# Weight blocks of a two-layer trunk step in two matmuls of 512 and 256 columns instead of three of 256

## The chip, the cores and the metric

The kernel runs on one core of one Trainium2 chip. The metric is the device time of one execution in microseconds; the median of three runs is given. The profile is that of one execution.

## What is computed

One inference step of a hybrid backbone with two layers over 128 context tokens and 128 latent tokens of width 2048, in float32. Each layer has a mixer (layer 0: differential attention beside a convolution module; layer 1: a state-space scan, S5, beside grouped attention) and a squared-ReLU MLP of width 8192, each behind a modulated RMS norm and with a gated residual. Cut to what matters here:

```python
def sq_relu_mlp(h, w1, w2):
    a = jax.nn.relu(h @ w1)
    return (a * a) @ w2

...
        xp = xp + gp1 * mp
        xs = xs + gs1 * ms
        xp = xp + gp2 * sq_relu_mlp(modulate(xp, norm_g[l, 1], sp2, cp2), mlp_w1[l], mlp_w2[l])
        xs = xs + gs2 * sq_relu_mlp(modulate(xs, norm_g[l, 1], ss2, cs2), mlp_w1[l], mlp_w2[l])
```

The linears are float32 products: the input and output projections of the mixers, the gate of the S5, and the two matrices of the MLP. The modulation (shift, scale and gate of each sub-layer) is a product of the conditioning vectors with a further weight matrix, `ada_w`.

## The kernel before

Activations lie transposed: 128 channels on the partitions, 256 columns (128 context tokens, then 128 latent tokens). A tile of 128 output channels is one linear. Its weights come as pieces of 128 x 1024 (eight blocks of 128 x 128), by SP's queue into eight `raw` buffers.

To keep float32 precision with the rounded type fp32r, every factor is split in two. `high` (line 359) rounds a weight piece on ACT into `wh`, `low` (line 364) has DVE subtract it from the piece into `wl`; there are four buffers of each. `put` (line 543) does the same with an activation tile: its high half goes to columns 0 to 255 of a tile `hl`, its low half to 256 to 511. A tile `hl` comes from a pool of 24 slots of 516 columns or, for part of the MLP's hidden activations, from the pool `hid`, whose tiles have 512 columns (line 549); in layer 1 all hidden tiles of the second quarter and the first eight of the others lie there, in layer 0 the first eight of each quarter (lines 1696, 1703, 1714).

`block` (line 453) is the product of one weight block with one activation tile, three matmuls into the same 256 columns of a PSUM bank:

```python
        mm(ps, w[0][:, s], x[:, 0:n], start=start, stop=False, **kw)
        mm(ps, w[0][:, s], x[:, n:2 * n], start=False, stop=False, **kw)
        mm(ps, w[1][:, s], x[:, 0:n], start=False, stop=stop, **kw)
```

`part` (line 460) runs it over the eight blocks of a piece, `linear` (line 476) over two pieces. There are other ways in: `staged` (line 482) runs a few linears side by side, first on one half of the activations; with 258 columns it serves the first linears of three norms (`enter`, line 769: 7, 5 and 7 linears), where two columns carry the shift. `pairs` (line 502) puts two linears in the halves of one bank (12 at the start of layer 0, 8 and 6 in the output projections). The gate of the S5 (`glu`, line 1192) has eight linears of eight blocks, every other one in a bank of the tag `ps`. `new` (line 472) hands out a bank of the tag `lin`, of which there are four, cut to 256 columns.

Results are taken out of PSUM by small strands: `copied` (line 557), `residual` (line 807: two DVE instructions that multiply by the gate and add to `x`, after a wait for the gate), `gated` (line 888: sigmoid of one linear times another), `u_tile` (line 1142), `glu_tile` (line 1179), `gqa_values` (line 1229), `gqa_head` (line 1253) and `squared_relu` (line 1735: ReLU on ACT into a tile `ms`, then one DVE product, then `put`).

The order of the instructions is planned. The program is many generators (strands). A first run, thrown away, keeps a clock for each engine by a table of costs (`charge`, line 136) and always goes on with a strand whose operands are there by then (`pick`, line 230); a second run issues in that order, loading and splitting weights ahead. `get` and `free` (lines 273, 285) count slots of named tags: four banks `lin`, three `ps`, three work tiles each of `h` and `xr`. Beside the linears run the modulation on TensorE (`ada`, line 569, in steps that fill gaps; `evict`, line 589, takes it out over a tile `ev`), two vectors of it on DVE (`ada_vector`, line 615, tile `va`, in both MLPs), the tables of the S5 (`s5_tables`, line 1404, in the first MLP: DVE products, transposes, DMAs from POOL's queue, `m2d` the last) and the convolution on DVE. Layer 0's MLP runs up and down projections by quarters; layer 1's runs up, up, down, down, up, down, up, down.

In time, the first mixer lasts to about 460 us, the first MLP to 1310, the second mixer to 1600, the second MLP to 2402, and the final norm ends the program.

Of the kernel before, what the change touches and what calls it, by code (L numbers as in the profile page):

```python
# [9 lines left out]
F32 = mybir.dt.float32  # L10
# [38 lines left out]
class Engine:  # L49
    """An engine whose instructions are also charged to the program's clocks."""  # L50
# [27 lines left out]
class Line:  # L78
    """A strand of the program: a generator that says what its next instructions wait for."""
# [4 lines left out]
    def on_pe(self):  # L84
        """Whether its next instructions are for TensorE."""
        return callable(self.wait) and getattr(self.wait, "pe", False)
# [25 lines left out]
class Kern:  # L112
    def __init__(self, ctx, tc, ins, outs, plan=None, order=None):
# [16 lines left out]
        self.cap = {"lin": 4, "ps": 3, "hl": 24, "h": 3, "xr": 3, "uv": 2}  # L130

# [1 line left out]
    # The program is many strands. A first run, that is thrown away, keeps a clock for each engine and always goes  # L133
    # on with a strand whose operands are there by then; the second run builds the program in that order, with
    # the weights loaded and split ahead of their use.
# [59 lines left out]
    def at(self, *aps):  # L195
        """When the tiles' contents are there."""
        return max([0] + [NEVER if v.tensor.name in self.held else self.at_.get(v.tensor.name, 0) for v in aps])

    def hold(self, t):
        """Not all of t is written yet."""  # L200
        self.held[t.tensor.name] = True
# [10 lines left out]
    def bulk(self, lead):  # L212
        """For work that is not urgent: the engines have come up to `lead` behind the clock of TensorE."""
# [59 lines left out]
    def get(self, *tags, on=None):  # L273
        """Waits for free slots (and for tiles), and takes them."""
# [55 lines left out]
    def source(self, spec):  # L330
        """The columns of a piece, side by side."""
# [38 lines left out]
    def pump(self, upto=0):  # L370
        """Loads ahead, as far as there is room, and splits what has come (and the pieces before `upto` in any
        case)."""
# [24 lines left out]
    def slot(self, key, bufs, back=0):  # L397
        """When the slot of the next tile (or one after it) is free."""
# [4 lines left out]
    def peek(self, n, split=False):  # L403
        """When the next n raw tiles are there."""
# [5 lines left out]
    def take(self, split, *spec):  # L410
        """The next piece that has been loaded: its halves, or itself."""
# [32 lines left out]
    def there(self, X, a, b, weights=True):  # L444
        """For a wait: the tiles X[a:b], and the weights that come next."""
# [7 lines left out]
    def block(self, ps, w, x, s, start, stop, **kw):  # L453
        mm = self.nc.tensor.matmul
        n = ps.shape[1]
        mm(ps, w[0][:, s], x[:, 0:n], start=start, stop=False, **kw)
# [3 lines left out]
    def part(self, ps, src, X, a, b, first, last, w=None, **kw):  # L460
        """ps (+)= weight blocks a to b of a tile times X[a:b]."""
# [10 lines left out]
    def new(self):  # L472
        yield from self.get("lin")
        return self.bank("lin")[:, 0:256]
# [7 lines left out]
    def staged(self, srcs, X, width, groups, done, release=None):  # L482
        """Linears in groups: first all on the half of X that is there first."""
        n = 0
# [1439 lines left out]
```

## Time and profile before

| what | before |
|---|---|
| runs, us | 2421.68, 2417.54, 2425.27 (median 2421.68) |
| profiled execution, span | 2417.9 us (the page gives no other time for it) |
| PE / weight loads / DVE / ACT / POOL busy | 96 / 88 / 70 / 48 / 7% of the span |
| matmuls, weight loads | 20152, 20152 |
| DMA moved | 627.64 MB, mean 260 GB/s |

Times within the execution are microseconds from the span's start. PE is TensorE's matmuls, PEld its weight loads, which run beside matmuls; the end of a matmul is modelled, so pitches are taken from one start to the next. All instructions of the kernel stand under one line (L60, the recording helper), so they are told apart by tile: `lin` is the bank that a linear writes, `wh` and `wl` the halves of its weights, `hl` of its activations.

### The profile page before, as it was taken

To read this page: it belongs to the slowest core of one execution; us is meant where nothing else is said; L and a number is where in the kernel's file an instruction comes from. 1 tells how busy PE (TensorE), PEld (TensorE's weight loads), DVE (VectorE), ACT (ScalarE), POOL (GpSimd) and SP (SyncE) were. 2 spreads that over 40 slices of the span, in tenths; PEclk is the share of its full clock that TensorE was granted. 3 is DMA by queue.
4 is the path that set the end of the run, shared out by engine and by line. 5 is a ranking of instruction groups with operands and counts; after the bars stand their busy time and mean duration, and the time that the engine had idled before them with its cause. 6 is when DMAs were issued, how large, how long until landed. Compare 5 with 4: busy or idle time off the path is not lost.

```text
span 2417.9 us, 49512 instructions
## 1 busy us (share of the span) xinstructions
PE 2331.7 (96%) x20152; PEld 2134.6 (88%) x20152; DVE 1696.8 (70%) x2957; ACT 1154.1 (48%) x1894; POOL 173.5 (7%) x293
## 2 busy tenths in 40 slices
PE   6999999999999999999999978999999999999997
PEld 1788887888999999999999857799999999999997
DVE  1489985677889898887666434566998855555555
ACT  2364457465444434434455644555744333443453
POOL 0000000000111011101000236000000000000000
PEclk9999999999999999999999988999999999999998
DMA  9979987879678898879877877765587855555552
GB/s 384 339 261 325 320 312 255 293 269 317 204 265 301 300 316 299 311 263 333 281 231 249 295 281 265 270 226 181 187 295 268 273 192 193 182 191 190 184 186 94
DMA packets 179638, 627.64 MB, mean 260 GB/s; under 512 B 21377, under 2 KB 21393, under 8 KB 179153
## 3 DMA queue, kind: packets, MB, share of 16 engines
q1 hardware_dynamic: 169920, 595.67, 71.1%
q0 software_dynamic: 9488, 28.81, 3.9%
q8 instruction: 158, 2.59, 0.4%
q14 instruction: 72, 0.58, 0.1%
HBM read 602.17 MB, written 26.41 MB: 260 GB/s over the span
## 4 chain that ended last, share of the span: by engine, by line
PE 85%; DVE 3%; DMA 3%; ACT 3%; POOL 3%; issue 1%; DVEq 0%; SPq 0%; ACTq 0%; POOLq 0%
PE lin L60 76%; PE ada L60 5%; POOL rt L60 2%; DVE wl L60 1%; DMA raw<-in_ada_w 1%; POOL hs L60 1%; ACT wh L60 1%; PE m1T L60 1%; DMA raw<-m3d 1%; ACT hs L60 0%; PE ps L60 0%; DMA raw<-in_ew_in 0%; PE po L60 0%; ACT L60 0%; DMA raw<-in_w 0%
## 5 line engine op out<-in xcount | busy, mean ns | idle before, releaser
L60 PE MATMUL lin<-hl,wh 128*128 128x256 f32 (+1 forms) x11200 | 2009.6, 282 | 7.2 <-ACT wh L60 7.0
L60 PEld LDWEIGHTS lin<-hl,wh 128*128 128x128 f32 x11200 | 1715.2, 189 | 98.4 <-issue 57.4
L60 PE MATMUL lin<-hl,wl 128*128 128x256 f32 (+1 forms) x5600 | 1569.9, 280 | 12.1 <-DVE wl L60 12.1
L60 PEld LDWEIGHTS lin<-hl,wl 128*128 128x128 f32 x5600 | 1058.2, 189 | 14.9 <-DVE wl L60 14.9
L60 DVE TENSOR_TENSOR wl<-raw,wh 128x1024 fp32r<-128x1024 f32 (+1 forms) x716 | 857.2, 1206 | 278.5 <-ACT wh L60 276.8
L60 ACT CAST wh<-raw 128x1024 fp32r<-128x1024 f32 (+1 forms) x716 | 738.6, 1035 | 520.0 <-PE lin L60 273.7
L60 PE MATMUL ada<-raw,condp 128*32 128x512 f32 (+1 forms) x1408 | 186.0, 572 | 19.5 <-DMA raw<-in_ada_w 19.3
L60 DVE SCALAR_TENSOR_TENSOR x<-lin,mod,x 128x128 f32<-128x128 f32 x320 | 97.1, 345 | 102.8 <-PE lin L60 102.6
L60 DVE SCALAR_TENSOR_TENSOR va<-raw,condp,va 128x1024 f32<-128x1024 f32 x120 | 148.4, 1277 | 0.0
L60 ACT ACTIVATE ms<-lin 128x256 f32<-128x256 f32 x114 | 43.8, 384 | 155.6 <-PE lin L60 155.6
L60 ACT CAST hl<-mq 128x256 fp32r<-128x256 f32 x128 | 51.8, 406 | 96.2 <-DVE mq L60 96.2
L60 DVE SCALAR_TENSOR_TENSOR cv<-cin,pke,cv 128x256 f32<-128x256 f32 x232 | 96.5, 476 | 0.0
L60 PEld LDWEIGHTS ada<-raw,condp 128*32 128x32 f32 x1408 | 32.8, 109 | 72.0 <-DMA raw<-in_ada_w 30.5
L60 DVE SCALAR_TENSOR_TENSOR mq<-lin,ms 128x256 f32<-128x256 f32 x114 | 47.9, 420 | 61.5 <-ACT ms L60 61.3
L60 ACT ACTIVATE sq<-x 128x256 f32<-128x256 f32 x75 | 31.0, 417 | 119.1 <-DVE x L60 117.1
L60 DVE TENSOR_TENSOR hl<-mq,hl 128x256 fp32r<-128x256 f32 x128 | 53.6, 421 | 28.3 <-ACT hl L60 28.1
L60 POOL TENSOR_TENSOR x<-x,rb 128x512 f32<-128x512 f32 (+1 forms) x2 | 4.2, 2133 | 916.6 <-ACT rb L60 916.6
L60 DVE TENSOR_TENSOR acc<-acc,sq 128x256 f32<-128x256 f32 x75 | 31.8, 424 | 32.2 <-ACT sq L60 30.4
L60 DVE TENSOR_TENSOR hl<-h,hl 128x256 fp32r<-128x256 f32 (+1 forms) x112 | 45.4, 420 | 9.1 <-ACT hl L60 8.7
L60 ACT CAST hl<-h 128x256 fp32r<-128x256 f32 (+1 forms) x112 | 42.8, 402 | 12.2 <-DVE h L60 11.5
L60 POOL DMA_DIRECT2D m3d<-m x32 | 21.6, 678 | 348.3 <-DVE m L60 347.1
L60 DVE TENSOR_TENSOR w<-s5z,bc 128x576 f32<-128x576 f32 x64 | 45.5, 752 | 0.6
(281 smaller groups left out, 1167.4 us busy)
## 6 DMA issues: line engine op xcount, KB each, us to landing
raw<-in_w SPq DMA_DIRECT2D x512, 512.0 KB, 5.1
raw<-in_ada_w SPq DMA_DIRECT2D x352, 512.0 KB, 6.1
raw<-in_ew_in SPq DMA_DIRECT2D x68, 512.0 KB, 6.0
raw<-in_ow_in SPq DMA_DIRECT2D x40, 512.0 KB, 6.5
raw<-in_ada_w SPq DMA_DIRECT2D x64, 256.0 KB, 6.2
raw<-in_ew_out SPq DMA_DIRECT2D x32, 512.0 KB, 6.2
raw<-in_ow_out SPq DMA_DIRECT2D x32, 512.0 KB, 4.7
m3d<-m POOLq DMA_DIRECT2D x32, 256.0 KB, 6.3
```

What stands on the lines that cost most here:

```text
L60: return f(out, *a, **kw)
```

## The change

`new`, the `staged` calls of the S5 input and of the MLP, and the S5 gate use a bank's whole 512 columns. `block` then issues two matmuls: the high weights over both activation halves into 512 columns, and the low weights over the high half into the first 256. The two halves of the result are added when it is taken out: ACT copies columns 256 to 511 to SBUF, DVE adds columns 0 to 255 (`add_halves`; `joined` does it into a work tile). The linears with 258 columns and those two to a bank stay as they were. `squared_relu` squares the joined tile in place with one DVE product; for the linears with 258 columns it no longer has a ReLU on ACT. `evict` now holds a lock `ev`. Left out below are comments that fall away and repetitions of the same edit.

```diff
-        self.cap = {"lin": 4, "ps": 3, "hl": 24, "h": 3, "xr": 3, "uv": 2}
+        self.cap = {"lin": 4, "ps": 3, "hl": 24, "h": 3, "xr": 3, "uv": 2, "ev": 1}
...
     def block(self, ps, w, x, s, start, stop, **kw):
         mm = self.nc.tensor.matmul
         n = ps.shape[1]
+        if n == 512:
+
+            mm(ps, w[0][:, s], x[:, 0:512], start=start, stop=False, skip_group_check=True)
+            mm(ps[:, 0:256], w[1][:, s], x[:, 0:256], start=False, stop=stop, skip_group_check=True)
+            return
...
     def new(self):
         yield from self.get("lin")
-        return self.bank("lin")[:, 0:256]
+        return self.bank("lin")
+
+    def add_halves(self, out, ps, release=None):
+
+        nc = self.nc
+        if ps.shape[1] != 512:
+            nc.scalar.copy(out, ps)
+        else:
+            nc.scalar.copy(out, ps[:, 256:512])
+            yield [out]
+            nc.vector.tensor_tensor(out, ps[:, 0:256], out, OP.add)
+        (release or self.free_lin)()
+
+    def joined(self, ps, release=None, tag="xr"):
+
+        yield from self.get(tag, on=[ps])
+        t = self.work.tile([128, 258], F32, name="sm", tag=tag, bufs=3)[:, 0:256]
+        yield from self.add_halves(t, ps, release)
+        yield [t]
+        return t
...
     def copied(self, dst, ps, note=None, release=None):
         yield [ps]
-        self.nc.scalar.copy(dst, ps)
-        (release or self.free_lin)()
+        yield from self.add_halves(dst, ps, release)
...
     def evict(self, ps, w, pieces):
-        yield from self.get("ps")
+        yield from self.get("ps", "ev")
...
     def residual(self, k, ps, l, i, summed, release=None, final=False):
         yield [ps]
+        two = ps.shape[1] == 512
+        if two:
+            ps = yield from self.joined(ps, release)
         yield self.mods((l, i, k // 8 * 8))
...
-        (release or self.free_lin)()
+        if two:
+            self.free("xr")
+        else:
+            (release or self.free_lin)()
...
             def gated(c, pa, pg, release_a=self.free_lin, release_g=self.free_lin):
-                nc.scalar.activation(g, pg, AF.Sigmoid)
-                release_g()
+                two = pa.shape[1] == 512
+                if two:
+                    pa = yield from self.joined(pa, release_a)
+                    yield from self.add_halves(g, pg, release_g)
+                    yield [g]
+                    nc.scalar.activation(g, g, AF.Sigmoid)
+                else:
+                    nc.scalar.activation(g, pg, AF.Sigmoid)
+                    release_g()
...
-            yield from self.staged([("ow_in", k) for k in range(5, 8)], h, 256, (3,), lambda n, ps: self.spawn(
+            yield from self.staged([("ow_in", k) for k in range(5, 8)], h, 512, (3,), lambda n, ps: self.spawn(
...
             def glu_tile(o, ps, tag):
-                nc.scalar.activation(g, ps, AF.Sigmoid, bias=self.pk["glu_b"][:, o:o + 1])
-                self.free(tag)
+                yield from self.add_halves(g, ps, lambda: self.free(tag))
+                yield [g]
+                nc.scalar.activation(g, g, AF.Sigmoid, bias=self.pk["glu_b"][:, o:o + 1])
...
     def gqa_head(self, r, pq, mix, mp, m2, qss, qn, rqs, kn, kx, vt, vcx, keys, vts):
+        pq = yield from self.joined(pq)
...
     def squared_relu(self, f, ps, hid, hp, release=None):
         nc = self.nc
-        yield from self.get("xr", "h", on=[ps])
-        s = self.work.tile([128, 258], F32, name="ms", tag="xr", bufs=3)[:, 0:256]
-        nc.scalar.activation(s, ps, AF.Relu)
-        yield [s]
+        if ps.shape[1] == 512:
+            q = yield from self.joined(ps, release, "h")
+            nc.vector.scalar_tensor_tensor(q, q, 0.0, q, OP.max, OP.mult)
+            yield from self.put(hid, f, q, hp)
+            self.free("h")
+            return
+        yield from self.get("h", on=[ps])
         q = self.work.tile([128, 258], F32, name="mq", tag="h", bufs=3)[:, 0:256]
-        nc.vector.scalar_tensor_tensor(q, ps, 0.0, s, OP.max, OP.mult)
-        (release or self.free_lin)()
-        self.free("xr")
+        nc.vector.scalar_tensor_tensor(q, ps, 0.0, ps, OP.max, OP.mult)
+        release()
         yield from self.put(hid, f, q, hp)
         self.free("h")
```

## Rows read from the trace of the kernel before

**Rows 1.** Page: busy time by engine; the chain that ended last, by line.

```profile
...
PE 2331.7 (96%) x20152; PEld 2134.6 (88%) x20152; DVE 1696.8 (70%) x2957; ACT 1154.1 (48%) x1894; POOL 173.5 (7%) x293
...
PE lin L60 76%; PE ada L60 5%; POOL rt L60 2%; DVE wl L60 1%; DMA raw<-in_ada_w 1%; POOL hs L60 1%; ACT wh L60 1%; PE m1T L60 1%; DMA raw<-m3d 1%; ACT hs L60 0%; PE ps L60 0%; DMA raw<-in_ew_in 0%; PE po L60 0%; ACT L60 0%; DMA raw<-in_w 0%
...
```

**Rows 2.** Timeline, PE, 2000 to 2004: start us, us, engine, line, operation, tiles.

```profile
...
2000.03 0.28 PE L60 MATMUL lin<-hl,wl 128*128 128x256 f32 x1
...
2003.77 0.28 PE L60 MATMUL lin<-hl,wl 128*128 128x256 f32 x1
...
```

**Rows 3.** Timeline, PE, 1740 to 1746.

```profile
...
1740.32 0.28 PE L60 MATMUL lin<-hl,wl 128*128 128x256 f32 x1
...
1745.98 0.28 PE L60 MATMUL lin<-hl,wl 128*128 128x256 f32 x1
...
```

**Rows 4.** Timeline, weight loads (PEld), 1684.5 to 1685.2.

```profile
...
1684.68 0.53 PEld L60 LDWEIGHTS nrm<-ones,acc 128*128 128x128 f32 x4
1685.14 0.19 PEld L60 LDWEIGHTS lin<-hl,wh 128*128 128x128 f32 x1
```

**Rows 5.** Groups by line, PE: count, busy us, mean ns of one, idle before.

```profile
...
L60 PE MATMUL lin<-hl,wh 128*128 128x256 f32 (+1 forms) x11200 | 2009.6, 282 | 7.2 <-ACT wh L60 7.0 <-DVE hl L60 0.2
...
L60 PE MATMUL lin<-hl,wl 128*128 128x256 f32 (+1 forms) x5600 | 1569.9, 280 | 12.1 <-DVE wl L60 12.1
...
```

**Rows 6.** Timeline, PE, 215.8 to 216.3.

```profile
...
215.85 0.59 PE L60 MATMUL rot<-qk,pke 128*128 128x256 f32 x2
...
```

**Rows 7.** Tile rot: count, duration ns min/median/max, first and last start us.

```profile
...
L60 PE MATMUL rot<-qk,pke x16: 377/379/380, 156.0 to 383.1; 128*128 128x256 f32 x16
...
```

**Rows 8.** Groups by line and shape: count, busy us, mean ns, idle.

```profile
...
L60 DVE TENSOR_TENSOR uv<-lin,rb 128x256 f32<-128x256 f32 x19 | 8.0, 420 | 3.1 <-PE lin L60 1.2 <-ACT h L60 1.1 <-ACT hl L60 0.2
...
L60 ACT COPY qk<-lin 128x256 f32<-128x256 f32 x16 | 5.9, 371 | 5.8 <-PE lin L60 5.6
...
```

**Rows 9.** Windows: PE, PEld, DVE, ACT, POOL busy us (count); clock, DMA share, GB/s.

```profile
...
0.00:597.00 597.00, 559.80 (x4477) 450.90 (x4478) 405.79 (x896) 306.05 (x595) 20.17 (x42) 0.99 0.88 307
717.00:1150.00 433.00, 432.75 (x3959) 404.09 (x3958) 378.37 (x576) 182.30 (x271) 55.85 (x91) 1.00 0.88 305
1150.00:1331.00 181.00, 181.00 (x1525) 168.58 (x1524) 122.24 (x221) 91.90 (x153) 0.73 (x1) 1.00 0.77 255
1731.00:1923.00 192.00, 191.76 (x1644) 190.12 (x1644) 177.68 (x208) 90.00 (x129) 0.00 (x0) 1.00 0.81 273
1923.00:2402.00 479.00, 478.75 (x4120) 478.54 (x4119) 272.30 (x358) 211.40 (x263) 0.00 (x0) 1.00 0.54 180
...
```

**Rows 10.** Windows, tile wl alone: PE, PEld, DVE; clock, DMA share, GB/s.

```profile
...
0.00:597.00 597.00, 315.08 (x1118) 212.17 (x1118) 174.44 (x154) 0.99 0.88 307
597.00:1331.00 734.00, 523.05 (x1872) 352.06 (x1872) 282.62 (x234) 1.00 0.82 280
717.00:1150.00 433.00, 303.44 (x1086) 204.03 (x1085) 165.42 (x138) 1.00 0.88 305
1331.00:1731.00 400.00, 208.22 (x735) 140.26 (x735) 111.73 (x91) 0.95 0.70 245
1731.00:1923.00 192.00, 149.84 (x536) 100.95 (x536) 82.68 (x69) 1.00 0.81 273
1923.00:2402.00 479.00, 382.68 (x1374) 258.83 (x1373) 205.74 (x169) 1.00 0.54 180
...
```

**Rows 11.** Tile m2d, the last of the S5 tables: durations, first and last start.

```profile
...
L60 POOL DMA_DIRECT2D m2d<-lgd x32: 563/566/597, 722.0 to 1110.9; - x32
...
```

**Rows 12.** Timeline, DVE, 1833 to 1846.

```profile
...
1833.60 0.42 DVE L60 SCALAR_TENSOR_TENSOR mq<-lin,ms 128x256 f32<-128x256 f32 x1
...
1838.93 0.42 DVE L60 SCALAR_TENSOR_TENSOR mq<-lin,ms 128x256 f32<-128x256 f32 x1
...
```

**Rows 13.** Chain of waits, 717 to 1150 by line; 1923 to 2418 by piece.

```profile
...
by line: PE lin L60 84.1%; PE ada L60 5.7%; PE m1T L60 2.5%; DMA raw<-in_w 2.2%; PE lgF L60 1.2%; DVE wl L60 1.0%; PE lgB L60 0.7%; issue 0.6%; DVE w L60 0.6%; DVE va L60 0.3%; ACT wh L60 0.2%; PE adv L60 0.2%; SPq L352 0.2%; DVE m1t L60 0.
...
1922.99 478.77 PE lin L60 x4120
...
```

More of the change, by code (lines that the diff above doesn't have):

```diff
@@ L600, in evict @@
                 nc.tensor.transpose(p2[:, c], ev[:, j * 128:(j + 1) * 128], self.ident)
+        self.free("ev")
         yield [p2]
@@ L895, in gated @@
                                         g.rearrange("p (s t) -> p s t", s=2), OP.mult)
-                release_a()
+                if two:
+                    self.free("xr")
+                else:
+                    release_a()
                 self.free("t1k")
@@ L1144, in u_tile @@
                 u = m2.tile([128, 256], F32, name="ut", tag="t1k", bufs=5)
-                nc.scalar.copy(u, ps)
-                release()
+                yield from self.add_halves(u, ps, release)
                 uts[k] = u
@@ L1195, in glu @@
                     yield from self.get(tag)
-                    ps = self.bank(tag)[:, 0:256]
+                    ps = self.bank(tag)
                     yield from self.part(ps, ("glu_w", o), yhl, 0, 8, True, True)
@@ L1232, in gqa_values @@
         vv = m2.tile([128, 256], F32, name="vvd", tag="t1k", bufs=5)
-        nc.scalar.copy(vv, ps)
-        self.free("lin")
+        yield from self.add_halves(vv, ps)
         yield from self.get("ps", on=[vv])
@@ L1260, in gqa_head @@
         nc.vector.tensor_scalar(q, pq, self.pk["qk_g"][:, 0:1], None, OP.mult)
-        self.free("lin")
+        self.free("xr")
         yield from self.get("ps", on=[sq])
@@ L1704, in mlp @@
                         fs = range(ahead, ahead + 3)
-                        yield from self.staged([("w1", l, f) for f in fs], h, 256, (3,), lambda n, ps: self.spawn(
+                        yield from self.staged([("w1", l, f) for f in fs], h, 512, (3,), lambda n, ps: self.spawn(
                             self.squared_relu(ahead + n, ps, hids[0], hp if ahead + n < 8 else None)))
```

## The prediction

> **What bounds the kernel now.** I read the page first. PE is busy 96% of the span, DVE 70%, ACT 48%, and three quarters of the chain that ended last are PE on the tile `lin` [rows 1]. So TensorE sets the end, and its weight matmuls are most of it. A busy PE says little on its own, so next I took pitches (start to start) from the timeline. In the second MLP the third matmul of a block starts at 2000.03, and that of the eleventh block after it at 2003.77: 340 ns a block, 113.3 ns a matmul [rows 2]. In another linear sixteen blocks last from 1740.32 to 1745.98: 354 ns [rows 3]. No wait stands in either stretch. The first reads activation tiles of the pool `hid`, 512 columns apart, the second slots of 516 columns (line 549), so I put the 14 ns down to where the moving operand starts.
>
> What is the 113 ns made of? The one-column matmuls of `nrm` load weights of the same shape, and four such loads take 0.53 us where one takes 0.19: (0.53 - 0.19) / 3 = 113 ns apart [rows 4]. With one column or 256 the pitch is the same: the weight load sets it, and the columns hide in it. So the load that the change leaves out is worth something.
>
> **What changes, in counts.** 5600 matmuls of `lin` read the low half of the weights [rows 5], and 32 more write banks of the tag `ps` (half of the S5 gate's), thus 5632 blocks. Unchanged by the code: 19 linears with 258 columns (304 blocks) and the 26 that lie two to a bank (12 + 8 + 6; 416 blocks). So 4912 blocks lose one matmul and one weight load. Of these, 1152 have their activation in `hid` (eight of sixteen tiles in the 64 down linears of layer 0; 40 of 64 tiles, sixteen outputs each, in layer 1), 3760 in 516-column slots. The linears concerned are 28 + 8 + 121 + 15 + 8 + 10 + 121 = 311.
>
> **The price of the new pair.** No row has a rounded matmul of 512 columns. From below: it can hardly be shorter than one load, 113 ns. From above: two of 256, 227 ns on `hid` tiles and 236 on the others, so that nothing is saved. The nearest row is `rot`, unrounded, 256 columns, whose pair takes 0.59 us [rows 6] where one takes 0.379 [rows 7]: 0.21 us pitch, a stream long enough to hide its load. I take 217 ns; none of its sixteen comes near the lower end. A block on `hid` is then 217 + 113 = 330, saving 10 ns. On 516-column slots the misplaced start should be paid once a read: 222 + 118 = 340, saving 14; at best it vanishes in the long read, 217 + 118 = 335, saving 19. In all 1152 x 10 + 3760 x 14 = 64 us at TensorE.
>
> Against this speaks one rule. The Trainium skill, "TensorE: Matmul & The Clock Gate", section Back-to-back issue gap, gives a warm gap of N/2.4 + 2.5 ns: by it a block goes from 327.5 to 325.0 ns, and the change saves 2.5 x 4912 = 12 us (an estimate from the page). The trace does not agree with it: it has 340 and 354, not 327.5, at a fully granted clock.
>
> **What it adds.** ACT copies a result's upper half, DVE adds the lower. The like rows: `qk` from `lin`, 371 ns on ACT; `uv` from `lin` and `rb`, 420 ns on DVE [rows 8]. DVE: 311 x 0.42 = 131 us on 1697. ACT: one copy for 146 residuals, 8 queries and 8 tiles of the S5 gate, two for 5 gates of the convolution, 172 x 0.371 = 64 us on 1154; in squared ReLU the copy takes the place of the ReLU. The add waits for the copy and the copy for PE's last matmul of the linear; behind the add on DVE stands the next weight split `wl`, for which PE waits. Today the same stands behind the squared ReLU and the residual, so I cost this wait at nothing where DVE has room, and in the stages below where it has none. Not hidden: where the next step waits for the last residual, at four places (two output projections, two MLP ends), 0.37 + 0.42 = 0.8 us each, 3 us. The lock on the tile `ev` concerns evictions of the modulation, far from their use: nothing. A residual now frees its bank before it waits for the gate, which can only help.
>
> **Stage by stage, what of the 64 us arrives.** The windows give each stage's load [rows 9] and its blocks, one `wl` matmul each [rows 10].
> - 0 to 597: 1118 less 432 unchanged, 686 blocks, 9.6 us. DMA is at 88% and PE has idle time; I take half, 4.8.
> - 717 to 1150: 1086 blocks, some 320 on `hid`, 13.9 us. DVE has 378 us of work, plus 68 linears x 0.42 = 407 of 433: 94%, and the stage wants to shrink. What fills DVE, the S5 tables and a vector of the modulation, may slide: the last table leaves at 1110.9 [rows 11], and from 1150 to 1331 DVE is at 68%. But their steps are long and stand in one queue with the splits. I take 0.6: 8.3.
> - The rest of 597 to 1331: 786 blocks less 40 of 258 columns, some 192 on `hid`, 9.7 us; at 0.85, 8.2.
> - 1331 to 1731: 735 less 248 unchanged, 487 blocks, 6.8 us; POOL's recurrence and DMAs hold the first half; 3.7.
> - 1731 to 1923: 536 blocks, 7.2 us. DVE 177.7 + 33.5 x 0.42 = 191.8 of 192: full. A linear with its two steps of `va` now takes DVE 1838.93 - 1833.60 = 5.33 us [rows 12], with the add 5.7, as long as sixteen blocks take PE today (16 x 0.354). 2.2 us, for what `va` slides.
> - 1923 to 2402: 1374 blocks, some 576 on `hid`, 17.0 us. The chain is PE alone for 479 us [rows 13], DVE at 57%. All of it.
>
> Sum 44 less 3: 41 us. The profiled span of 2417.9 becomes 2377; the median of the runs, 2421.7, stands 3.8 above that span, so **2381 us**, 1.7% less.
>
> **Rivals.**
> 1. *All of it arrives*: 19 ns on the 516-column slots, tables and `va` slide without a wait: 11.5 + 71.4 - 3 = 80 us, 2342. For it: from 717 to 1150 the chain is PE for over nine tenths [rows 13]. Against: DVE's sums above.
> 2. *The pitch goes with the columns*: the 113 is a stream's rate, the long matmul takes 227 to 236, nothing is saved and the 3 us are added: 2425. For it: the tile's place matters, so the moving read does; against it, the one-column rows.
> 3. *DVE becomes the bound, and it is slower.* Place: 717 to 1150 and 1731 to 1923. If the DVE shares seen today (87.4% and 92.6%) are all that its queue reaches, since its head waits for ACT's copy and that for PE, the stages take 407 / 0.874 = 466 (+33) and 191.8 / 0.926 = 207 (+15); the others give back 34 - 3: 17 us slower, 2439. It decides when DVE stays under 598.8 / 655.7 = 91% over both. Against it: today these stages wait for PE, not for DVE, so the shares are no ceiling, and in [rows 12] DVE runs without a gap.
>
> That the change does not do what it says is little likely: `block` branches on the tile's width alone, and `new` hands out 512.
>
> **Numbers.** Forecast 0.65 (its own range 2355 to 2408; the upper end has the long matmul halfway to 227, so half of the savings, and nothing from the two stages where DVE is full: 34 / 2 - 3 = 14 us), rival 1 0.18, rival 2 0.09, rival 3 0.08. The range, 2337 to 2410, takes in forecast and rival 1 and leaves out rivals 2 and 3. A measurement of this kernel tells about 0.3%, 7 us, from no change. Faster by more: forecast and rival 1, 0.83. Within: most of rival 2, 0.07. Slower: rival 3 and what rival 2 has beyond 7 us, 0.10.
>
> **What would show it.** Right: 15240 matmuls instead of 20152; some 330 ns a block on `hid` tiles, 340 on others; 17 us less from 1923 to the end; over 90% DVE in the stage of the tables, and these ending later than 1111. Wrong: blocks still at 340 and 354 (rival 2); PE waiting for `wl` in the two full stages by more than 20 us in sum (rival 3); a long matmul clearly under 217 ns, which would put the time under my range.

## The result, and the profile after

The changed kernel takes 2455.91 us (median of four runs, 2452.06 to 2458.95) against 2420.56 for the kernel before, run beside it: a ratio of 1.0145, 95% interval 1.0127 to 1.0162, so 35 us slower. The forecast was 2381, the range 2337 to 2410. The profiled execution has a span of 2450.3 us, 32.4 more than before.

The page of the changed kernel, busy time by engine, then its groups (columns as in [rows 5]):

```profile
PE 2337.3 (95%) x15240; PEld 1905.1 (78%) x15240; DVE 1804.6 (74%) x3268; ACT 1191.1 (49%) x2051; POOL 169.0 (7%) x293
...
L60 PE MATMUL lin<-hl,wh 128*128 128x512 f32 (+2 forms) x6320 | 2008.7, 373 | 10.9 <-ACT wh L60 9.5
L60 PE MATMUL lin<-hl,wl 128*128 128x256 f32 (+1 forms) x5600 | 1577.9, 282 | 27.7 <-DVE wl L60 27.4
...
L60 DVE TENSOR_TENSOR sm<-lin,sm 128x256 f32<-128x256 f32 x273 | 114.8, 421 | 139.9 <-ACT sm L60 139.7
```

Against [rows 1, 5]: a quarter of the matmuls and of the weight loads is gone, as counted, DVE has 108 us more work (1804.6 - 1696.8; an add takes the 421 ns that were reckoned), and PE is as busy as before, 2337 us against 2332. PE's waiting for `wl` went from 12.1 to 27.4 us, of which 23.2 stand in the second mixer (1327 to 1718). So the work left out bought no time; the timeline (PE, second MLP, tiles of `hid`, the counterpart of [rows 2]) shows it in the pitch:

```profile
2035.97 0.28 PE L60 MATMUL lin<-hl,wl 128*128 128x256 f32 x1
2036.10 0.40 PE L60 MATMUL lin<-hl,wh 128*128 128x512 f32 x1
2036.34 0.28 PE L60 MATMUL lin<-hl,wl 128*128 128x256 f32 x1
2036.45 0.39 PE L60 MATMUL lin<-hl,wh 128*128 128x512 f32 x1
2036.68 0.28 PE L60 MATMUL lin<-hl,wl 128*128 128x256 f32 x1
...
2039.86 0.28 PE L60 MATMUL lin<-hl,wl 128*128 128x256 f32 x1
```

A long matmul holds the place for 240 and 230 ns (2036.10 to 2036.34, 2036.45 to 2036.68), and the eleven blocks from 2035.97 to 2039.86 take 353.6 ns each. Before, it was 340. On the slots of 516 columns (sixteen blocks, counterpart of [rows 3]) there is a small gain, 5.59 / 16 = 349 ns against 354:

```profile
1772.02 0.28 PE L60 MATMUL lin<-hl,wl 128*128 128x256 f32 x1
...
1777.61 0.28 PE L60 MATMUL lin<-hl,wl 128*128 128x256 f32 x1
```

With these the sum of the prediction reads 3760 x 4.6 - 1152 x 13.6 = 1.6 us instead of 64, if all blocks on `hid` had stood at 340. A count over the whole trace says the same: from one block to the next it is 351.5 ns on average before and 351.6 after (starts of successive matmuls on `wl` with nothing but `lin` between them, steps over 420 ns left out; 5368 and 5366 steps), since before only some 900 of the steps take 340. The pair is worth nothing in sum, and over 30 us are lost besides. Where, the sums of the four norms between the stages tell (tile `nrm`: durations, first and last start); four rows of before, then of after:

```profile
L60 PE MATMUL nrm<-ones,acc x4: 250/250/271, 506.2 to 506.5; 128*128 128x1 f32 x4
L60 PE MATMUL nrm<-ones,acc x4: 250/250/271, 1314.1 to 1314.4; 128*128 128x1 f32 x4
L60 PE MATMUL nrm<-ones,acc x4: 168/250/250, 1684.8 to 1685.1; 128*128 128x1 f32 x4
L60 PE MATMUL nrm<-ones,acc x4: 250/250/271, 2403.4 to 2403.7; 128*128 128x1 f32 x4
```

```profile
L60 PE MATMUL nrm<-ones,acc x4: 169/250/250, 520.6 to 520.9; 128*128 128x1 f32 x4
L60 PE MATMUL nrm<-ones,acc x4: 165/250/250, 1327.6 to 1327.9; 128*128 128x1 f32 x4
L60 PE MATMUL nrm<-ones,acc x4: 164/250/250, 1717.9 to 1718.1; 128*128 128x1 f32 x4
L60 PE MATMUL nrm<-ones,acc x4: 250/250/271, 2435.7 to 2436.0; 128*128 128x1 f32 x4
```

| stage | before, us | after, us | difference |
|---|---|---|---|
| first mixer (to the first of these sums) | 506.2 | 520.6 | +14.4 |
| first MLP | 807.9 | 807.0 | -0.9 |
| second mixer | 370.7 | 390.3 | +19.6 |
| second MLP | 718.6 | 717.8 | -0.8 |

A mixer is counted here with its output projection, up to the next norm's sum, so the first one ends at 506 and not at about 460. Both MLPs, where the forecast had most of its gain, last as long as before; both mixers are longer. In the first one, the convolution ends late: its norm sum comes at 379.7 instead of 359.5 (tile `nrm` again, before and after), and the windows of 200 to 300 us show why it could (PE, PEld, DVE, ACT, POOL busy; clock, DMA share, GB/s): VectorE, which does the convolution, was already busy for 91% of them.

```profile
L60 PE MATMUL nrm<-ones,cacc x4: 165/250/250, 359.5 to 359.7; 128*128 128x1 f32 x4
200.00:300.00 100.00, 100.00 (x814) 82.20 (x807) 91.45 (x191) 46.07 (x79) 6.48 (x12) 1.00 0.92 326
```

```profile
L60 PE MATMUL nrm<-ones,cacc x4: 250/250/272, 379.7 to 380.1; 128*128 128x1 f32 x4
200.00:300.00 100.00, 100.00 (x607) 71.88 (x606) 92.08 (x195) 46.61 (x84) 6.45 (x12) 1.00 0.91 323
```

The adds that fall before its end, ten of gates and eighteen of heads at 0.42 us, are at most 12 of the 20 us; the rest would be waiting, since an add stands at the head of VectorE's queue until ScalarE's copy is there. That share is argued here and was not measured by itself.

In the second mixer the attention's first scores come at 1526.4 instead of 1477.6 (tile `sc`). Of these 49 us about 13 come from ahead: the second key's copy starts at 1408.2 instead of 1395.6. ScalarE's timeline shows where the others arise; first before, then after:

```profile
1395.64 0.38 ACT L60 COPY kn<-lin 128x256 f32<-128x256 f32 x1
1396.05 0.42 ACT L60 ACTIVATE ksq<-kn 128x256 f32<-128x256 f32 x1
...
1407.57 3.89 ACT L60 COPY hn<-hs 64x1024 f32<-64x1024 f32 x2 [3.85 <-POOL hs L60]
...
L60 PE MATMUL sc<-kn,qs x16: 272/275/583, 1477.6 to 1548.3; 128*128 128x128 f32 x16
```

```profile
1408.20 0.38 ACT L60 COPY kn<-lin 128x256 f32<-128x256 f32 x1
...
1418.93 3.88 ACT L60 COPY hn<-hs 64x1024 f32<-64x1024 f32 x2 [6.51 <-POOL hs L60]
...
1423.72 0.42 ACT L60 ACTIVATE ksq<-kn 128x256 f32<-128x256 f32 x1
1443.08 1.07 ACT L60 COPY ys<-y 128x512 f32<-128x512 f32 x2 [18.94 <-issue]
...
L60 PE MATMUL sc<-kn,qs x16: 272/275/377, 1526.4 to 1576.0; 128*128 128x128 f32 x16
```

Before, the second key is copied and squared at once, ahead of `hn`, the hand-over of the state-space scan, which waits for POOL. After, an add on VectorE stands between copy and square; the planner has put `hn` into the gap, so the square waits behind it, misses its turn, and the key's norm goes on behind the scan's outputs (`ys`, then the norm sum on PE at 1446.8). The output projection needs the attention's half first.

### The profile page after: what moved, and what is told of

Same layout as the page of the kernel before. It is cut to its first block, busy times and chain, and to the rows that moved or that the text cites. A ratio compares the mean times of both kernels' runs of the same rounds, so it can differ in the third digit from the quotient of the medians.

```text
span 2450.3 us, 40178 instructions
## 1 busy us (share of the span) xinstructions
PE 2337.3 (95%) x15240; PEld 1905.1 (78%) x15240; DVE 1804.6 (74%) x3268; ACT 1191.1 (49%) x2051; POOL 169.0 (7%) x293
## 4 chain that ended last, share of the span: by engine, by line
PE 86%; DMA 4%; ACT 3%; POOL 3%; DVE 3%; issue 2%; DVEq 0%; SPq 0%; ACTq 0%; POOLq 0%
PE lin L60 77%; PE ada L60 5%; POOL rt L60 2%; DMA raw<-in_ada_w 1%; DMA raw<-in_ew_in 1%; ACT wh L60 1%; DVE wl L60 1%; POOL hs L60 1%; ACT hs L60 1%; PE m1T L60 1%; PE sc L60 0%; PE po L60 0%; DMA raw<-m3d 0%; DVE acc L60 0%; DMA pk<-in_pack 0%
## 5 line engine op out<-in xcount | busy, mean ns | idle before, releaser
L60 PE MATMUL lin<-hl,wh 128*128 128x512 f32 (+2 forms) x6320 | 2008.7, 373 | 10.9 <-ACT wh L60 9.5
L60 PE MATMUL lin<-hl,wl 128*128 128x256 f32 (+1 forms) x5600 | 1577.9, 282 | 27.7 <-DVE wl L60 27.4
L60 PEld LDWEIGHTS lin<-hl,wh 128*128 128x128 f32 x6320 | 1143.5, 189 | 304.8 <-issue 41.0
L60 ACT COPY sm<-lin 128x256 f32<-128x256 f32 x273 | 101.7, 373 | 407.9 <-PE lin L60 394.0
L60 DVE TENSOR_TENSOR sm<-lin,sm 128x256 f32<-128x256 f32 x273 | 114.8, 421 | 139.9 <-ACT sm L60 139.7
L60 PE MATMUL ada<-raw,condp 128*32 128x512 f32 (+1 forms) x1408 | 191.1, 582 | 22.4 <-DMA raw<-in_ada_w 22.3
L60 ACT CAST hl<-sm 128x256 fp32r<-128x256 f32 x114 | 46.3, 406 | 116.7 <-DVE sm L60 116.7
L60 DVE SCALAR_TENSOR_TENSOR x<-sm,mod,x 128x128 f32<-128x128 f32 x292 | 89.2, 347 | 3.1
L60 DVE TENSOR_TENSOR hl<-sm,hl 128x256 fp32r<-128x256 f32 x114 | 48.0, 421 | 29.8 <-ACT hl L60 29.5
L60 DVE SCALAR_TENSOR_TENSOR sm<-sm 128x256 f32<-128x256 f32 x114 | 48.0, 421 | 2.0
```

Of the source, the lines that this page charges most:

```text
L60: return f(out, *a, **kw)
```

## The experiments

All times are medians; "before" is the kernel before, run beside each on the same chip (2420.9 to 2422.3 us).

### What a pair costs (e1, e5, e13)

Three kernels issue nothing but streams of rounded matmuls from tiles already in SBUF. The first compares widths, and the triple with the pair:

```diff
+    run("qte", triple, 512, 0, 16)     # distance of tiles, their shift, the weights' shift
+    run("qpe", pair, 512, 0, 16)
+    run("qlong", only(512), 512)
+    run("qhalf", only(256), 512)
```

> A kernel of matmul streams alone, 48 blocks each, all operands in SBUF before it starts; its time is not compared. Theory A (the pitch goes with the columns: the changed kernel's long matmul starts 231 to 236 ns before the next, twice the 116 to 118 of a short one): 512 columns alone about 231, 384 about 173, 256 alone 113 to 118, 128 and 64 clearly under 113; three matmuls and the pair take the same 340 to 354 a block at every place of the tiles. Theory B (the prediction's: the weight load sets 113 ns and columns hide in it): 512 columns about 217, and 128, 64 and 2 columns all at 113; the pair 10 ns or more under the three. On the place of the moving tile: if it explains 340 against 354, tiles 512 columns apart give 340 and tiles 520 columns apart 354 with three matmuls; if it does not, both are equal here.

Measured, by tile (streams that begin with L21 are triples, L26 pairs, L31 a single width; starts over 47 steps, which are blocks or pairs of matmuls), with two lines of the timeline (start, us) and one window:

```profile
L21 PE MATMUL qta<-mx,mw x48: 283/283/283, 28.4 to 45.3; 128*128 128x256 f32 x48
...
L21 PE MATMUL qte<-mx,mw x48: 275/276/276, 164.0 to 180.0; 128*128 128x256 f32 x48
...
L26 PE MATMUL qpe<-mx,mw x48: 388/397/398, 180.3 to 196.9; 128*128 128x512 f32 x48
...
L31 PE MATMUL qlong<-mx,mw x48: 389/389/398, 265.1 to 286.5; 128*128 128x512 f32 x48
...
315.09 0.25 PE L32 MATMUL qtwo<-mx,mw 128*128 128x2 f32 x1
...
317.44 0.28 PE L31 MATMUL qtwo<-mx,mw 128*128 128x2 f32 x1
...
L31 PE MATMUL qbfl<-mxb,mwb x48: 379/379/390, 409.8 to 430.1; 128*128 128x512 bf16 x48
...
L31 PE MATMUL qbfh<-mxb,mwb x48: 272/273/273, 430.5 to 440.8; 128*128 128x256 bf16 x48
...
334.00:353.00 19.00, 19.00 (x91) 19.00 (x91) 0.00 (x0) 0.00 (x0) 0.00 (x0) 0.50 0.00 1
```

512 columns take 21.4 / 94 = 228 ns (233 on tiles 520 columns apart), and 384 took 173: from 256 columns up the pitch of rounded matmuls goes with the columns, 0.44 to 0.47 ns each, where theory A put 231, and the prediction's 217 is excluded. 256 columns took 120 ns alone (`qhalf`, 11.3 / 94) and 340 / 3 = 113 in the triple of `qte`, and 113 is just what [rows 4] gave for a weight load. The two limits meet there; that is why the one-column rows could not tell them apart. Narrower ones get no shorter: two columns take 112 ns each at full clock (21 of them from 315.09 to 317.44, granted 1.00), which is a load alone, as theory B had it. Then the clock fell, while the engine did only narrow matmuls, to 0.50 granted, the 1.2 GHz level; there 64 columns (20.0 / 94) and 128 both take 213 ns, and 512 take 427 (`qsamel`, two of them from 375.12 to 375.97). So at both levels a load lasts about as long as 256 columns, and theory A's "128 and 64 clearly under 113" did not come.

The bf16 streams take 216 and 109 ns. The rule that the prediction weighed, N/2.4 + 2.5 (the Trainium skill, "TensorE: Matmul & The Clock Gate", Back-to-back issue gap), gives 215.8 and 109.2: the trace agrees with it for bf16, and rounded float32 is 4 to 10% above it (113 to 120 ns at 256 columns, 228 at 512).

The pair takes 353 ns (16.6 / 47) at both places, the triple 360 in `qta` and 340 in `qte`, where only the weights have been shifted by 64 bytes. So theory A failed in this: the place does matter, for the triple. The distance of the tiles alone is not it: 512 columns apart gave 360, 520 apart 355. The next kernel shifts tiles and weights:

```diff
+    for o in (0, 8, 16, 24, 32, 40, 48, 56, 64, 96, 128, 192, 256, 384, 448):
+        run(f"sx{o}", triple, 512, o, blocks=24)
+    for o in (0, 8, 16, 32, 48, 64, 128):
+        run(f"spx{o}", pair, 512, o, 16, blocks=24)
```

> Streams alone again, 24 blocks each: three matmuls a block while the moving tiles, the weights, or both are shifted by some columns of 4 bytes (the name of a bank gives the shift: sx moving tile, sw weights, sxw moving tile with the weights shifted by 16, sl the low weights alone, st the distance of the moving tiles, spx the pair with the weights shifted by 16). The first streams showed 340 a block with the weights shifted by 16 columns, 353 to 360 at five other places, and the pair at 349 to 355 everywhere. Theory A (the phase between the place of weights and of moving tile sets it): 340 comes back at several shifts of either, with a period, and the pair stays between 349 and 356 at all seven of its places. Rival (the place of the moving tile alone, as the prediction had it): the sw streams all like one another, the sx streams not. Rival (the pair has good places too, which the kernel misses): one of the spx streams at 341 or less.

The timeline (first matmuls of a stream and of the next one) for twice the same place, weights shifted by 64 bytes:

```profile
165.47 0.28 PE L21 MATMUL sw<-mx,mw 128*128 128x256 f32 x1
...
173.95 0.28 PE L21 MATMUL sw<-mx,mw 128*128 128x256 f32 x1
...
276.44 0.28 PE L21 MATMUL sxw<-mx,mw 128*128 128x256 f32 x1
...
284.60 0.28 PE L21 MATMUL sxw<-mx,mw 128*128 128x256 f32 x1
```

24 blocks take 8.48 us the first time, 353 ns each, and 8.16 the second, 340. The rivals both fall (the weights' place matters as well, and no pair came under 350), but theory A is not the whole either: one place has two speeds. Shifts of the moving tile by 64, 128, 192, 256, 384 and 448 columns, all multiples of 256 bytes, left it at 360, like no shift at all; that is why the later runs count places modulo 256 bytes. The kernel before agrees: its blocks on `hid` stood at 340 in some linears and 353 in others. The third kernel asked what chooses:

```diff
+            steps(triple, "rset", 96, 6)
+            single(p)
+            steps(triple, kind + "one" + L[i], own, 16)
```

> Streams alone: sixteen blocks on tiles 64 (names m...) or 192 (names n...) bytes off the weights' place modulo 256, after six blocks at 96 and then one block (blk, pair) or one matmul (one) at 0, 32, 64, 96, 128, 160, 192 or 224 (last letter a to h); keepa to keepe ask whether the state lasts over modulation-like matmuls and shorter ones. In the kernel before, blocks on hid (64 off) took 340 after a slot at 224, and 353 after slots at 32, 64 or 96. Theory A (the stream keeps one of two states at one place, 340 or 353, and the step from the tile before chooses): mblkh at 340 from its second block on, mblkb, mblkc and mblkd at 353; one matmul alone chooses as well as a block; the pair is at 349 to 356 in all sixteen of its streams, so there is nothing for it to win. Rival (the pair has the lower state too, and the changed kernel merely fell into the upper one): one of the pair streams at 341 or less. Rival (the state comes from something outside, other engines or the bank): mblkh at 353 here.

By tile, after one matmul at 0 (`monea`) and at 224 (`moneh`), and the pair (`mpairh`); 15 blocks each:

```profile
L23 PE MATMUL monea<-mx,mw x16: 279/279/279, 87.8 to 93.1; 128*128 128x256 f32 x16
...
L23 PE MATMUL moneh<-mx,mw x16: 276/276/276, 143.3 to 148.4; 128*128 128x256 f32 x16
...
L26 PE MATMUL mpairh<-mx,mw x16: 387/397/398, 207.6 to 212.9; 128*128 128x512 f32 x16
```

353, 340 and 353 ns. The triple keeps one of two states through a whole stream; the pair has no lower one: its sixteen streams begin with blocks of 343 to 358 and average 349 to 354. That is the part of theory A that matters here. Its other part missed: a whole block at 224 led to 353, one matmul to 340, so the tile before does not choose by itself. On tiles 64 bytes off the weights' place one of sixteen triple streams came to 340, on tiles 192 off eleven. What chooses stays open.

### Where the loss lies (e3, e4, e2)

`new` hands out 512 or 256 columns by the linear's source, and results of 256 columns leave as before:

```diff
-        return self.bank("lin")
+        return self.bank("lin") if wide(src) else self.bank("lin")[:, 0:256]
```

> The pair with its adds in the two MLPs alone; the mixers' linears have three matmuls of 256 columns and are taken out as before. Theory A (both MLPs of the changed kernel last as long as before, all of the loss is in the mixers): 2415 to 2427, as before. Rival (the loss is spread with the adds over the whole kernel, by the share of the linears): 242 of the 311 linears are here, so 2440 or more.

> The reverse: the pair and its adds in the two mixers alone, MLPs as before. Theory A: all of the loss, 2448 to 2462. Rival (spread over all linears): 69 of 311 linears, 2430 or less.

MLPs alone: 2426.6, ratio 1.0025 (1.0015 to 1.0034). Mixers alone: 2458.6, ratio 1.0159 (1.0142 to 1.0176). So 78% of the changed linears cost 6 us and the other 22% cost 38: the loss is in the mixers. The two do not add up to 35, and where the 6 arise is open.

```diff
+        if n == 512 and THREE:
+            mm(ps[:, 0:256], w[0][:, s], x[:, 0:256], start=start, stop=False, skip_group_check=True)
+            mm(ps[:, 256:512], w[0][:, s], x[:, 256:512], start=False, stop=False, skip_group_check=True)
+            mm(ps[:, 0:256], w[1][:, s], x[:, 0:256], start=False, stop=stop, skip_group_check=True)
```

> The changed kernel with its 512-column banks, copies and adds, but with three matmuls of 256 columns a block (the two high ones into the two halves of the bank). Theory A (the pair as such gains and loses nothing in sum, what costs are the adds): 2456 within 8. Rival (the pair saves TensorE time on most tiles, and the loss of the adds is larger than 34 us): over 2470. Rival (the long matmul is what costs, in the blocks on 512-column tiles, 11 ns each): under 2447.

2445.5, ratio 1.0104 (1.0089 to 1.0119), 10 us less than with the pair. The rival with the dear long matmul had the number, but not the place: of the 6.5 us between the profiled spans (2443.8 and 2450.3) the first mixer has all (its norm sum comes at 514.1, not 520.6), and the second MLP, full of `hid` tiles, 2.8 that the second mixer and the first MLP give back. It shows that the pair gains nothing: 25 of the 35 us are there with three matmuls too. Why the first mixer likes three better is open; it is not the pitch, which averages 353.3 ns a block there with three matmuls and 352.0 with the pair.

### Which chains (e6 to e10)

The same switch, now with single groups of linears narrow and everything else as in the changed kernel. A narrow linear is rid of the add and of the long matmul at once; only e2, which keeps the adds, tells the two apart.

> The changed kernel, but the two key linears of the second mixer keep three matmuls of 256 columns and one copy. Theory K (the add makes the second key miss its turn before the state-space scan's outputs: its norm sum came at 1447 instead of 1398, the first scores at 1526 instead of 1477, and the output projection waits for them): the scores come 30 us or more earlier and the time falls to 2436 to 2444. Rival (the second mixer's 20 us are spread over all its adds): the scores still begin after 1515, and 2451 or more.

Two linears of 311: 2441.1 us, 15 less, theory K. The second key is squared at 1407.3 and the scores begin at 1489.3:

```profile
L60 ACT ACTIVATE ksq<-kn x2: 418/418/418, 1399.3 to 1407.3; 128x256 f32<-128x256 f32 x2
...
L60 PE MATMUL sc<-kn,qs x16: 272/275/582, 1489.3 to 1563.0; 128*128 128x128 f32 x16
```

In e2, with the add and three matmuls, the second key is as late as in the changed kernel: squared at 1417.4, behind `hn` at 1412.6. So it is the add that does it, and not the long matmul:

```profile
L60 ACT ACTIVATE ksq<-kn x2: 416/417/418, 1395.1 to 1417.4; 128x256 f32<-128x256 f32 x2
...
L60 PE MATMUL sc<-kn,qs x16: 273/275/377, 1522.7 to 1572.5; 128*128 128x128 f32 x16
```

> The changed kernel, but the ten linears that gate the convolution's input keep three matmuls of 256 columns, with sigmoid and product straight from PSUM. Theory L (VectorE's load before the end of the convolution sets the first mixer's loss of 14 us: ten gate adds and eighteen head adds of 0.42 us): 4 to 6 us less than the changed kernel, 2450. Rival (the convolution gets its inputs late, by the longer chain copy, add, sigmoid, product): 10 to 14 us less, 2442 to 2446.

> The changed kernel, but the attention heads' linears of the first mixer (eighteen of them in the changed form) keep three matmuls of 256 columns and one copy. Theory L: 7 to 10 us less, 2446 to 2449. Rival (late inputs of the convolution): within 3 us of the changed kernel, 2453 or more.

2452.8 (1.0134, 1.0115 to 1.0153) and 2449.7 (1.0117, 1.0102 to 1.0132): a gain of 3 and 6 us, each less than theory L said, and the first rival's 10 to 14 did not come either; the gain of 3 is not clear of the noise, since the intervals of e7 and of the changed kernel overlap. The convolution's norm sum came earlier by 8.3 and 7.2 us (371.4 and 372.5 against 379.7), but in the profiles the mixer ended as late as in the changed kernel, at 520.2 and 519.9. Single profiles scatter by a few us: that of the changed kernel is of its shortest run, that of e8 of its longest. Neither group seems enough alone, so both together with the keys:

> The changed kernel, but the gates and the attention heads of the first mixer and the two keys of the second keep three matmuls of 256 columns and their old way out; both output projections, the rest of the second mixer and both MLPs have the pair. Theory (the 33 us are three late chains: the convolution's end, put off by 18 us through the gate adds and the head adds together, either alone giving back only half of it and nothing of the mixer's end; and the second key's missed turn, 15 us): the convolution's norm sum comes again at 359 to 363 us, the first mixer ends within 4 us of before (506), and the time is 2422 to 2430. Rival (the output projections' adds or the first mixer's own load carry the first 14 us): the first mixer still ends at 515 or later, 2437 or more.

2425.6, ratio 1.0016 (1.0005 to 1.0027): 30 of the 35 us are back. By tile `nrm`:

```profile
L60 PE MATMUL nrm<-ones,cacc x4: 165/250/250, 360.6 to 360.8; 128*128 128x1 f32 x4
...
L60 PE MATMUL nrm<-ones,acc x4: 169/250/250, 510.8 to 511.0; 128*128 128x1 f32 x4
L60 PE MATMUL nrm<-ones,acc x4: 168/250/250, 1315.2 to 1315.4; 128*128 128x1 f32 x4
L60 PE MATMUL nrm<-ones,acc x4: 166/250/250, 1688.7 to 1688.9; 128*128 128x1 f32 x4
```

The first mixer keeps 4.6 us (0.6 more than the theory allowed), the second 2.8 (373.5 against 370.7). The lock and the shorter squared ReLU without the pair:

```diff
-        yield from self.get("ps")
+        yield from self.get("ps", "ev")
```

> The kernel before with what else the change touches and nothing of the pair: the lock on the tile of the modulation's evictions, and squared ReLU in one product, without the ReLU on ScalarE, for the nineteen linears with 258 columns. Theory: nothing, 2417 to 2425. Rival (these make up the 6 us by which the MLPs-only version stands above before): 2425 to 2430.

2422.5, ratio 1.0002 (0.9991 to 1.0012): nothing, as the prediction had it for the lock. Its profile has the first mixer end at 509.2, 3.0 later than before, without any pair; so e9's 4.6 and 2.8 us are little more than the scatter of single profiles.

### Can the lower state be held? (e11, e12, e14 to e16)

If three matmuls could be kept at 340 everywhere, TensorE would gain in the kernel before about what the change was forecast to. The edits move the activation slots:

```diff
-RAW = 8
+RAW, SLOT = 8, 544
...
-        t = (pool or self.hlp).tile([128, 512 if pool else 516], F32R, name="hl", tag="hl")
+        t = (pool or self.hlp).tile([128, 512 if pool else SLOT], F32R, name="hl", tag="hl")
```

> The kernel before with three matmuls, its activation slots 544 columns apart in place of 520 (516 rounded up), so that all of them begin 64 bytes off the weights' place modulo 256, as the tiles of hid do; room is made by packing the padded conditioning vectors and the pick matrix closer. The arithmetic is unchanged. Theory (the phase between weights and moving tile, modulo 256 bytes, decides: 340 on hid, 354 on slots whose phase goes round): the linears on slots go to 340 a block, 14 ns on some 3760 blocks and 720 narrower ones, of which the stages bound by TensorE give back most: 2375 to 2395. Rival (340 or 353 is a matter of how a stream falls in, as the streams alone showed both at one and the same place): the slots stay at 353 to 354, 2417 to 2425.

> As the one before, but slots 576 columns apart, so that all have the same phase and not two in turn; for the room one buffer of raw weights less, seven instead of eight. Theory (phase decides): 340 a block on all slots; 2375 to 2400, less what the missing buffer costs where the loads bound (the first mixer, the first MLP). Rival (turn of the phases does not matter, or the place does not): the same block time as with 544.

2431.8 (1.0047, 1.0032 to 1.0062) and 2443.9 (1.0096, 1.0080 to 1.0112): both slower, so the theory fell. 544 columns are 2176 bytes, eight and a half times 256, so the slots lie 64 and 192 bytes off in turn and not all at 64, as the first expectation had it; and the second MLP lost even the 340 that it had on `hid` (353 a block on average, no step at 340). With 576 the slots lie 192 bytes off the weights' place modulo 256, not 64. There 631 of 1935 steps in the first MLP take 341 ns or less, before 337 of 1955. For the next, the tiles of `hid` are shifted as well (`hpad`, 32 columns), and then a matmul is put ahead of each linear:

```diff
+            self.pool("hpad", 1, stack=st).tile([128, 32], F32, name="hpad")
...
+        if start and n == 256 and not kw:
+            mm(ps, w[0][:, s], x[:, 16:272], start=True, stop=True)
```

> The kernel of the run with slots 576 columns apart, three matmuls a block, with the tiles of hid moved by 128 bytes as well, so that every activation tile begins 192 bytes off the weights' place modulo 256; there eleven of sixteen streams alone fell into the lower state, at 64 off one of sixteen. Theory (the lower state is kept wherever all places are alike and 192 off): 340 a block through both MLPs, 13 ns on some 4000 blocks, so 2390 to 2410 against 2444. Rival (it depends on the last step into each stretch, and the MLPs fall into the upper state as they did at 64): 353 a block, 2440 to 2447.

> As the one before, with one more matmul ahead of each linear of 256 columns, on the first tile shifted by 64 bytes; its result is overwritten by the first real one. In the streams alone one matmul 64 bytes on, before tiles at 192, led to 340. Theory: 340 in every linear, for one more matmul of 113 ns in sixteen blocks: 6 ns a block given back of 13, 2405 to 2425 whatever the run before shows. Rival (the kernel's own breaks undo it, or the shift leads to the upper state as often): 353 a block and 35 us more than the run before or about 2475.

> The kernel with slots 544 columns apart (places 64 and 192 off in turn, all eight raw buffers) and the same additional matmul ahead of each linear. Theory (both places hold the lower state once in it): 340 a block on slots and on hid, 16 x 13 less 113 ns for each of some 300 linears, 2395 to 2415 against 2432. Rival (the turn of the two places brings the upper state back): 353 a block, 2455 to 2467.

2438.3 (1.0064, 1.0047 to 1.0081), 2469.9 (1.0196, 1.0181 to 1.0211) and 2464.0 (1.0170, 1.0155 to 1.0185): the theory's times missed three times, and the rivals' are right to within 6 us. The blocks, though, did not all stay at 353. With all places alike 1268 of 1928 steps in the first MLP take 341 ns or less, with the matmul ahead 1500 of 1839; in the second MLP it is 344 of 2002 and 278 of 1891, where the kernel before has 563 of 2013. On slots 544 apart the matmul ahead brought 13 steps of 1855 in the first MLP and none in the second. An example of the first MLP of e14 (9 blocks from 1119.88 to 1122.94, 340 ns), and its window from 717 to 1150 (columns and counterpart in [rows 9]):

```profile
1119.88 0.28 PE L60 MATMUL lin<-hl,wl 128*128 128x256 f32 x1
...
1122.94 0.28 PE L60 MATMUL lin<-hl,wl 128*128 128x256 f32 x1
...
717.00:1150.00 433.00, 426.96 (x3984) 397.58 (x3983) 376.90 (x581) 180.60 (x272) 58.34 (x95) 1.00 0.88 303
```

The first MLP still lasted 811.2 us against 807.9 (norm sums at 509.6 and 1320.8). PE was busy for 801.8 us of it against 807.6, so the shorter blocks saved 6 us on TensorE, and 9 us of waiting, 5.9 of them for `wl` where it had 0.2, took them back. Shorter blocks did not make this stage shorter. The missing raw buffer may have its part in that; it was not tried alone. No version beats the kernel before.

## Why the prediction was wrong

- **The counts** were right: 15240 matmuls, 421 ns an add, and the last table leaves at 1278.8, later than 1111 as foreseen and without harm.
- **"The weight load sets the pitch, the columns hide in it"**: this step failed, and with it the whole gain. The 113 ns of [rows 4] are the price of a load (two columns take 112, e1), but a lower bound only; 256 rounded columns cost as much (113 to 120, e1), and 512 twice that. Leaving a load out of a stream whose columns take as long buys nothing. Rival 2 had said so, and got 0.09.
- **The 217 ns of the long matmul** came from `rot`, an unrounded stream [rows 6, 7], as the nearest row. Measured are 230 to 240 in the kernel and 228 to 233 alone; `rot`'s rate is that of 512 columns in bf16 (216, e1), and rounded float32 does not reach it. The upper bound named in the text, 227 to 236, was the answer.
- **340 for all slots, 330 on `hid`**: the 14 ns between the places were put down to where the moving tile starts. The same place shows both 340 and 353 (e5, e13), the weights' place counts too, and the pair has only the upper state. So `hid` lost 13.6 ns a block where it had stood at 340, and the slots won 4.6 in the stretch shown.
- **The adds "at nothing where DVE has room"**, looked for in two stages that were full: the place was wrong. The stage of `va` did fill up (185 of 191 us, 1765 to 1956 in the profile after, against [rows 9]), and the second MLP still lasted 718 us. PE waited there for no split, and for 1.6 us in the stage of the tables (730 to 1165), where rival 3's sign was 20 in sum. The loss came in the mixers, of which the prediction took VectorE's share as one mean (406 of 597 us, a window that reaches 91 us into the MLP). In the slice 200 to 300 us it is at 91%, with the convolution in it, and the output projection waits for the convolution. Shown by e9 with e7 and e8: with gates and heads narrow the convolution ends at 360.6 and the mixer at 510.8. Not all of it is the adds': with the adds and three matmuls (e2) the mixer ended at 514.1, 6.5 us earlier than with the pair, and that part stays open.
- **"The add waits for the copy, behind it stands the next split"** named the queue's head, but not who else gets past: the missed step is that an added wait lets the planner put other work into the gap, so the term put at nothing was not nothing. One key's square slid behind the scan's hand-over, 15 us for two linears (e6), and the same with three matmuls a block (e2).
- **3 us exposed at four places** was not tested by itself: with the three groups narrow the median stands 3 us above before (2425.6 against 2422.3), and what makes these up is not shown.
- **Rival 3** had the sign and half of the loss (2439), by a mechanism that did not act: neither MLP is longer.

## What to carry to other kernels

Before leaving out a weight load, ask what the columns beside it cost at the same operand type: where both limits are equal, removing one moves nothing, and a row at one column shows only one of them. Work added to the way out of a linear is priced at the consumers that wait for a particular result, slice by slice, and not by the engine's mean share; two of 311 linears carried 15 of the 35 us. In an order planned by a cost table, a new wait is also a gap into which something longer may be put.

## What the runs showed that had not been expected

Three rounded matmuls a block can run in one of two steady states, 340 or 353 ns, at one and the same place of their tiles and the same granted clock (1.00); shifts of a few columns of either operand change it (340 to 360), and a stream keeps its state for as long as nothing disturbs it. One matmul more before it can turn it. A block of 512 and 256 columns averages 348 to 354 at every place tried. Rounded float32 takes 228 ns for 512 columns where bf16 takes 216. And a stage in which TensorE was busy all the time did not get shorter when its blocks did (e14, with one raw buffer less): waits, most of them for the next split, took back what the blocks gave.
